# A third PSUM bank, taken from the projections' pair, for the chunked scan of a two-layer hybrid decoder

## The chip, the core and the metric

One core of one Trainium2 chip runs the whole program. The metric is device time in microseconds (us) of one execution. Engines are called PE (TensorE; PEld is its weight load), DVE (VectorE), ACT (ScalarE), POOL (GpSimd) and SP (SyncE, which issues the DMAs). Matmul results go into eight PSUM banks of 128 x 512 float32, named `B[0]` to `B[7]` in the kernel.

## The reference

Two layers over 512 tokens of width 1024. Each layer is

```
h   = rms_norm(x);  z, xbc, dt, sb_qkv, moba_qkv = split(h @ w_in)
xbc = silu(causal_conv(xbc));  dt = softplus(dt + bias);  xs, B, C = split(xbc)
per chunk c of 128 tokens, per head:
    y_diag  = ((C_c B_c^T) * L_c) (xs_c * dt_c)          # L_c: masked decays
    y_off   = (C_c state) * exp(acum_c)
    state   = state * chunk_decay_c + B_c^T (decay_to_end_c * dt_c * xs_c)
y_ssd = rms((y_diag + y_off + d_skip * xs) * silu(z)) * gain   # two groups
x  = x + rms_norm(concat(y_ssd, y_stickbreak, y_moba) @ w_out)
x  = x + rms_norm((silu(h2 @ w_gate) * (h2 @ w_up)) @ w_down), h2 = rms_norm(x)
```

The chunked scan (the Mamba-2 part, 8 heads of 64, two groups, state 128) runs over four chunks; the state is carried from chunk to chunk.

## The kernel before, in words

Every float32 projection is done as three matmul passes over a high and a low part of each operand; `split` makes these parts with one copy on ACT (L116) and one subtraction on DVE (L117). The weights come in 512 KB chunks through three raw buffers (DMA L131) and rings of four high and four low buffers (`wh`, `wl`).

All tiles are persistent; the eight banks are handed out by hand. A framework puts the instructions of each engine into an order at compile time, from priorities (program order, raised by `high_priority(offset=...)`) and simulated times. After that the order of an engine's queue is fixed; semaphores make an instruction wait for the data it reads, and for the earlier users of the bank or buffer it writes. So an instruction at the head of a queue that waits for a bank holds everything behind it on its engine.

The order of the work around the change, once in each layer:

- The MoBA attention (L431 to L464) writes logits into `B[3]`, their transposes into `B[4]` and its result into `B[2]`; L459 reads that out.
- The xBC projection (L475 to L482) and the Z projection (L483, matmuls at L212, silu on ACT at L156) take `B[0]` and `B[1]` in turn from the ring `acc`. Counting the takes of a layer (8 by the query-key pairs, 1 by dt, 8 by xBC), Z's token blocks 0 to 3 get `B[1]`, `B[0]`, `B[1]`, `B[0]`.
- The scan (L486 to L554), for each chunk c, takes banks from the ring `mx`: px (transposes of x, L501, read on DVE by L505, L506 and, but for the last chunk, L508), pb (transposes of B, L511, read by ACT L512; not in the last chunk), pc (C B^T, L515, read by L517), po (L531, read by L533; not in chunk 0) and pst (the state, L538, read by L541 or L544; not in the last chunk). That is 4, 5, 5 and 3 takes, 17 in all. The diagonal part (L525) always goes to `py = B[2]`, read by L527. L522 multiplies the decays by C B^T on DVE, L534 adds the two parts, L545 multiplies by silu(z), L549 squares on ACT, L164 takes a power on POOL, and L553 writes the chunk's result `MIX[c]`.
- The output projection (L559 to L591) works on token pairs with the banks `OB = (B[5:7], [B[7], B[0]], B[1:3], B[3:5])`. For token block j, `OB[j][0]` first holds the transposes of `MIX[j]`, `OB[j][1]` those of the attention results `MIXA[j]` (L577), which `split` moves to `RR`; then the matmuls of L565 accumulate in the two banks. So half of the matmuls of block j must wait until `MIX[j]` is done and its transposes have been read out. Pair 0 takes the weight chunks 4 to 7 first, then 0 to 3.
- Then comes the feed-forward part (L599 on): seven-product matmuls at L624, and the down projection at L691.

The scan has a priority offset of 100 instructions, the weight splits one of 800, the transposes for the output projection one of 4000.

Of the kernel before, what the change touches and what calls it, by code (L numbers as in the profile page):

```python
# [58 lines left out]
def trunk(ctx, tc, x, wch, wdt, gains, mixgain, conv, small, ident_d, consts_d, stack_d, out):  # L59
# [18 lines left out]
    B = [ps.tile([P, 512], F32, name=f"B{i}") for i in range(8)]  # L78
# [14 lines left out]
    def ring(items):  # L93
        n = [0]

        def take():
            n[0] += 1
            return items[(n[0] - 1) % len(items)]
        return take
# [171 lines left out]
    for l in range(DEPTH):  # L271
# [159 lines left out]
        mx = ring([B[3], B[4]])  # L431
# [51 lines left out]
        tok_proj(l, C_Z, acc, lambda t, p: silu(ZS[t], p))  # L483


        mx = ring(B[3:5])  # L486
        py = B[2]
        state = F[38]
        for c in range(NT):
# [281 lines left out]
```

## Time and profile before

| | |
|---|---|
| times of 3 runs | 1236.29, 1240.74 and 1318.46 us, median 1240.74 |
| profiled execution | 1236.18 us, its span 1234.4 us |
| mean granted clock of PE | 0.998 |
| busy in the span | PE 98%, PEld 88%, DVE 71%, ACT 49%, POOL 4% |

The profile is of one execution. Its span runs from the first to the last instruction; 1.8 us of its time lie outside. The third run, 1318.46 us, stands apart from the two others. Layer 0's scan lies at 186 to 236 us of the span, layer 1's at 794 to 844 us, with the same order of instructions.

### The profile page before, as it was taken

How to read it: one execution, taken by the hardware profiler on the slowest of the kernel's cores; microseconds unless marked ns; L12 is line 12 of the kernel's file. 1: busy time of each engine (PE TensorE's matmuls, PEld its weight loads, DVE VectorE, ACT ScalarE, POOL GpSimd, SP SyncE). 2: the span in 40 equal slices, each digit the busy share in tenths (PEclk: the TensorE clock that was granted, in tenths of full speed). 3: DMA queues.
4: the chain of work that ended last, by engine and by line, in shares of the span. 5: the costliest groups of instructions: out<-in, count | busy, mean ns of one | idle time of the engine just before them, and what ended most of it. 6: DMA issues, size and time to landing. Idle time of an engine off the chain costs nothing.

```text
span 1234.4 us, 19083 instructions
## 1 busy us (share of the span) xinstructions
PE 1206.0 (98%) x7558; PEld 1081.0 (88%) x7558; DVE 872.0 (71%) x1523; ACT 600.4 (49%) x1124; POOL 53.3 (4%) x88
## 2 busy tenths in 40 slices
PE   6999999999999999999999999999999999999997
PEld 5877888889999999888887888888899999998886
DVE  5456865879899998534555577478898899883343
ACT  5556664466444444433445666535654444453231
POOL 1010000010000000000110100001100000000000
PEclk9999999999999999999999999999999999999999
DMA  7322233242333333333323322132523333333321
GB/s 246 119 74 98 87 103 103 70 144 81 101 105 104 113 108 104 122 100 119 130 86 110 125 80 77 70 95 70 170 71 103 107 112 106 103 108 115 101 70 69
DMA packets 40778, 128.94 MB, mean 104 GB/s; under 512 B 5456, under 2 KB 5744, under 8 KB 40688
## 3 DMA queue, kind: packets, MB, share of 16 engines
q1 hardware_dynamic: 39344, 123.49, 30.6%
q0 software_dynamic: 1344, 4.23, 1.0%
q8 instruction: 59, 0.97, 0.3%
q14 instruction: 31, 0.25, 0.1%
HBM read 123.47 MB, written 4.23 MB: 103 GB/s over the span
## 4 chain that ended last, share of the span: by engine, by line
PE 81%; DVE 8%; DMA 5%; ACT 3%; issue 2%; POOL 0%; SPq 0%; DVEq 0%; POOLq 0%; ACTq 0%
PE B L624 22%; PE B L691 19%; PE B L221 15%; PE B L212 7%; PE B L565 6%; DMA wr<-in_wch_dram 4%; DVE wl L117 3%; ACT wh L116 2%; PE B L340 2%; DVE RR L650 1%; PE B L347 1%; PE B L453 1%; PE B L318 1%; PE B L525 1%; PE B L319 1%
## 5 line engine op out<-in xcount | busy, mean ns | idle before, releaser
L117 DVE TENSOR_TENSOR wl<-wr,wh 128x1024 fp32r<-128x1024 f32 (+1 forms) x198 | 220.0, 1114 | 85.8 <-ACT wh L116 84.4
L116 ACT ACTIVATE wh<-wr 128x1024 fp32r<-128x1024 f32 (+1 forms) x198 | 190.9, 966 | 151.3 <-PE B L624 88.0
L221 PE MATMUL B<-hT,wh 128*128 128x512 f32 (+1 forms) x768 | 215.7, 362 | 3.5 <-ACT F L307 2.2
L624 PE MATMUL B<-hT,wh 128*128 128x256 f32 x960 | 192.5, 283 | 0.6 <-ACT F L662 0.6
L624 PE MATMUL B<-D,wh 128*128 128x256 f32 x960 | 182.7, 283 | 0.6 <-DVE F L676 0.3
L691 PE MATMUL B<-wh,RR 128*128 128x512 f32 x608 | 164.8, 389 | 0.0
L624 PEld LDWEIGHTS B<-hT,wh 128*128 128x128 f32 x960 | 158.2, 192 | 1.0 <-ACT F L662 1.0
L221 PEld LDWEIGHTS B<-hT,wh 128*128 128x128 f32 x768 | 136.4, 191 | 23.6 <-ACT F L307 3.3
L624 PEld LDWEIGHTS B<-D,wh 128*128 128x128 f32 x960 | 153.2, 192 | 1.2 <-DVE F L676 0.7
L221 PE MATMUL B<-hT,wl 128*128 128x512 f32 (+1 forms) x384 | 137.7, 360 | 0.0
L624 PE MATMUL B<-hT,wl 128*128 128x256 f32 x480 | 136.2, 284 | 0.5 <-DVE wl L117 0.5
L624 PE MATMUL B<-D,wl 128*128 128x256 f32 x480 | 135.5, 283 | 0.0
L691 PEld LDWEIGHTS B<-wh,RR 128*128 128x128 f32 x608 | 114.0, 188 | 23.5
L116 ACT ACTIVATE wh<-RR 128x512 fp32r<-128x512 f32 (+1 forms) x120 | 85.8, 766 | 100.2 <-DVE RR L650 70.3
L117 DVE TENSOR_TENSOR RR<-F,RR 128x512 fp32r<-128x512 f32 x48 | 33.1, 691 | 103.7 <-ACT RR L116 103.7
L117 DVE TENSOR_TENSOR wl<-RR,wh 128x512 fp32r<-128x512 f32 (+1 forms) x120 | 101.1, 865 | 6.3 <-ACT wh L116 2.7
L691 PE MATMUL B<-wl,RR 128*128 128x512 f32 x304 | 95.4, 389 | 0.0
L624 PEld LDWEIGHTS B<-hT,wl 128*128 128x128 f32 x480 | 92.1, 192 | 1.0 <-DVE wl L117 1.0
L624 PEld LDWEIGHTS B<-D,wl 128*128 128x128 f32 x480 | 92.1, 192 | 0.0
L116 ACT ACTIVATE RR<-F 128x512 fp32r<-128x512 f32 x48 | 30.0, 629 | 125.9 <-PE B L691 124.7
L212 PE MATMUL B<-wh,hT 128*128 128x512 f32 x256 | 82.8, 399 | 0.9 <-DVE hT L117 0.9
L221 PEld LDWEIGHTS B<-hT,wl 128*128 128x128 f32 x384 | 73.0, 190 | 8.8
(206 smaller groups left out, 2004.3 us busy)
## 6 DMA issues: line engine op xcount, KB each, us to landing
wr<-in_wch_dram SPq DMA_DIRECT2D x204, 512.0 KB, 3.5
x<-in_x_dram SPq DMA_DIRECT2D x16, 256.0 KB, 3.2
F<-in_gains_dram SPq DMA_DIRECT2D x16, 256.0 KB, 4.4
F<-acd POOLq DMA_DIRECT2D x16, 256.0 KB, 6.3
xsave<-x SPq DMA_DIRECT2D x8, 256.0 KB, 2.0
x<-xsave SPq DMA_DIRECT2D x8, 256.0 KB, 3.3
out_dram<-x SPq DMA_DIRECT2D x8, 256.0 KB, 2.0
D<-in_mixgain_dram SPq DMA_DIRECT2D x4, 256.0 KB, 4.4
```

What stands on the lines that cost most here:

```text
L116: A.activation(hi, src, AF.Copy)
L117: return eng.tensor_tensor(lo, src, hi.bitcast(F32), op=OP.subtract)
L212: T.matmul(p, hT[a][:, k, t * P:(t + 1) * P], w[k // 2][b][:, (k % 2) * 512:(k % 2 + 1) * 512], start=n == 0, stop=n == 3 * KT - 1)
L221: T.matmul(p[:, t0 * P:t1 * P], w[b][:, k * P:(k + 1) * P], hT[a][:, k, t0 * P:t1 * P], start=first and n == 0, stop=n == 3 * KT - 1, skip ...
L318: T.matmul(p, tiles[2 + h][:, cs], tiles[h][:, cd], start=True, stop=False, skip_group_check=True)
L319: T.matmul(p, tiles[2 + h][:, cs], tiles[4 + h][:, cd], start=False, stop=stop, skip_group_check=True)
L340: T.matmul(pz[:, o:w], ntri if i2 == i else nones, s2, start=False, stop=i2 == NT - 1 and n == 1, skip_group_check=True)
L347: T.matmul(pv[:, j * 64:(j + 1) * 64], e[:, (j - i) * P:(j - i + 1) * P], VT[i][:, h * 64:(h + 1) * 64], start=i == NT - 1, stop=i == 0 an ...
L453: T.matmul(pv[:, h * 64:(h + 1) * 64], pTs[:, i * P:(i + 1) * P], VT[i][:, 256 + h * 64:256 + (h + 1) * 64], start=h == 0 and i == 0, stop ...
L565: T.matmul(OB[j][hf], lt, w[b][:, hf * 512:(hf + 1) * 512], start=k == ks[0] and a == 0 and b == 0, stop=k == ks[-1] and a == 1)
L624: T.matmul(p, w[b][:, half * 512 + k * P:half * 512 + (k + 1) * P], left(j, a, k), start=first and k == 0 and n == 0, stop=k == 3 and n == ...
L691: T.matmul(B[2 * t + hf], gs[a][:, t * P:(t + 1) * P], w[b][:, hf * 512:(hf + 1) * 512], start=i == 0 and a == 0 and b == 0, stop=i == HT ...
```

## The change

The ring that hands out banks to px, pb, pc, po and pst gets three banks instead of two:

```
-        mx = ring(B[3:5])
+        mx = ring([B[3], B[4], B[1]])
         py = B[2]
```

`B[1]` is one of the two banks of the ring `acc`, which the Z projection uses just before, and it is `OB[2][0]`, which takes the transposes of `MIX[2]` afterwards. No instruction is added or removed. What each take gets, in the order of the program:

```
chunk 0        px pb pc pst       before  3 4 3 4      after  3 4 1 3
chunk 1        px pb pc po pst    before  3 4 3 4 3    after  4 1 3 4 1
chunk 2        px pb pc po pst    before  4 3 4 3 4    after  3 4 1 3 4
chunk 3        px pc po           before  3 4 3        after  1 3 4
```

## Rows read from the trace of the kernel before

**Rows 1.** The page: span, busy times, and PE in 40 slices.

```profile
span 1234.4 us, 19083 instructions
...
PE 1206.0 (98%) x7558; PEld 1081.0 (88%) x7558; DVE 872.0 (71%) x1523; ACT 600.4 (49%) x1124; POOL 53.3 (4%) x88
...
PE   6999999999999999999999999999999999999997
```

**Rows 2.** Windows: stretch, length, busy us of PE PEld DVE ACT POOL, clock, DMA.

```profile
184.00:204.00 20.00, 20.00 (x116) 17.17 (x115) 8.24 (x13) 11.82 (x21) 0.17 (x1) 1.00 0.14 42
204.00:214.00 10.00, 10.00 (x59) 8.80 (x58) 8.57 (x14) 3.44 (x8) 1.52 (x2) 1.00 0.76 234
214.00:222.00 8.00, 8.00 (x51) 7.00 (x50) 6.67 (x11) 1.48 (x5) 0.00 (x0) 1.00 0.01 2
222.00:229.00 7.00, 6.10 (x42) 5.19 (x42) 7.00 (x15) 1.01 (x4) 1.07 (x1) 1.00 0.01 1
229.00:246.00 17.00, 17.00 (x90) 14.28 (x90) 13.93 (x23) 8.98 (x21) 1.40 (x2) 1.00 0.38 125
...
830.00:837.00 7.00, 6.14 (x42) 5.27 (x43) 7.00 (x15) 0.90 (x3) 1.07 (x1) 1.00 0.00 0
```

**Rows 3.** Waits of PE's weight loads, 184 to 246 us: us in total, times, longest.

```profile
PEld B L538 <- DVE F L517: 0.9, 1, 0.9
PEld B L531 <- DVE F L506: 0.5, 1, 0.5
PEld B L565 <- DVE RR L117: 0.3, 2, 0.2
PEld B L577 <- DVE F L517: 0.2, 1, 0.2
```

**Rows 4.** Timeline of PE, 222 to 229 us: start, us; idle before in brackets.

```profile
222.76 1.13 PE L538 MATMUL B<-D,D 128*128 128x256 f32 x4 [0.68 <-DVE F L517]
...
227.22 1.13 PE L531 MATMUL B<-D,F 128*128 128x256 f32 x4 [0.22 <-DVE F L506]
...
228.75 0.50 PE L565 MATMUL B<-wh,RR 128*128 128x512 f32 x1
```

**Rows 5.** Timeline of DVE and PE, 234 to 246 us: the last chunk and the last transposes.

```profile
235.03 0.68 DVE L533 TENSOR_TENSOR D<-B,SM 128x512 f32<-128x512 f32 x1
...
245.32 0.60 PE L577 MATMUL B<-ident,F 128*128 128x128 f32 x4
```

**Rows 6.** Timeline of DVE, 195 to 226 us.

```profile
195.75 0.42 DVE L517 TENSOR_TENSOR F<-B,cst 128x256 f32<-128x256 f32 x1 [3.54 <-PE B L515]
196.21 1.29 DVE L522 TENSOR_TENSOR F<-F,F 128x512 f32<-128x512 f32 x2
199.58 2.58 DVE L117 TENSOR_TENSOR wl<-wr,wh 128x1024 fp32r<-128x1024 f32 x2 [2.08 <-ACT wh L116]
...
214.23 0.69 DVE L533 TENSOR_TENSOR D<-B,SM 128x512 f32<-128x512 f32 x1 [1.19 <-PE B L531]
...
217.00 0.69 DVE L117 TENSOR_TENSOR RR<-B,RR 128x512 fp32r<-128x512 f32 x1 [0.69 <-ACT RR L116]
...
225.10 0.87 DVE L553 SCALAR_TENSOR_TENSOR F<-F,SM,D 128x256 f32<-128x256 f32 x2
```

**Rows 7.** Timeline, 195 to 207 us: bank users of chunks 0 and 1.

```profile
195.10 0.61 PE L515 MATMUL B<-F,F 128*128 128x128 f32 x4
...
197.12 0.60 ACT L156 ACTIVATE F<-B 128x512 f32<-128x512 f32 x1 [1.23 <-PE B L212]
...
200.94 0.61 PE L501 MATMUL B<-ident,F 128*128 128x128 f32 x4
...
201.80 0.39 ACT L512 ACTIVATE D<-B 128x256 f32<-128x256 f32 x1 [0.89 <-PE B L511]
...
202.41 0.68 DVE L505 TENSOR_TENSOR D<-B,SM 128x512 f32<-128x512 f32 x1
...
206.15 1.89 PE L525 MATMUL B<-D,F 128*128 128x64 f32 x16
```

**Rows 8.** Windows, columns as in rows 2, at a drop of the clock.

```profile
707.00:709.50 2.50, 1.30 (x6) 1.02 (x7) 1.83 (x2) 2.45 (x8) 0.00 (x0) 1.00 0.22 33
709.50:713.50 4.00, 4.00 (x12) 3.17 (x11) 2.14 (x3) 1.81 (x3) 0.00 (x0) 0.57 0.28 111
```

## Prediction

> **What bounds the kernel now.** I read first the page [rows 1]: PE is busy in 98% of the span, 1206.0 of 1234.4 us, and only its first and last slices fall below 9 tenths. The change neither adds nor removes an instruction, so PE's work stays; all that a bank can give back is time in which PE stands idle for want of one. Over the whole span PE is idle for 1234.4 - 1206.0 = 28.4 us, and most of that cannot belong to the scan, since the first and the last slice, of 30.9 us each, alone lack some 4 and 3 tenths, together about 20 us.
>
> The second view is busy time by stretch over the scan and the output projection of layer 0 [rows 2]. The reader should see that PE is full from 184 to 222 us and from 229 to 246 us, and that it lacks time only from 222 to 229 us: 6.10 of 7.00 us, while DVE is busy for all of the 7.00 us. Layer 1 shows the same at 830 to 837 us, 6.14 of 7.00 us. So the loss that the scan makes visible is 0.90 us in layer 0 and 0.86 us in layer 1, 1.8 us of the kernel.
>
> The third view is the waits of PE's weight loads in this stage [rows 3], which begin earlier than the matmuls and so count more: 0.9 + 0.5 + 0.3 + 0.2 = 1.9 us a layer. The timeline [rows 4] shows what the two largest are. L538 of chunk 2 (the state, bank 4) waits for L517 to read C B^T out of the same bank. L531 of chunk 3 (bank 3) waits for L506 to read px out of the same bank. Neither reads what L517 or L506 writes: these are waits for a bank and not for data. L577 (0.2 us) waits for bank 4 in the same way. The 0.3 us of L565 are waits for data, the split of the transposes.
>
> **The change part by part.**
>
> *The three bank waits go.* After the change, pst of chunk 2 goes to bank 4, whose user before is pb of the same chunk, and pc goes to bank 1; L538 reads what L512 makes out of pb anyhow, so its bank costs it nothing more. po of chunk 3 goes to bank 4 after L544 of chunk 2, whose result it needs anyhow. L577 for `MIXA[3]` must then wait for L533 of chunk 3 to free bank 4. That is at 235.03 + 0.68 = 235.7 us [rows 5], where it was ready at 228. Its result is wanted by pair 1, whose last transposes stand at 245.32 us [rows 5]; some 9 us of pair 0's matmuls hide the move, and if they did not, one split (0.69 us, the RR split in [rows 6]) would be bare. Removed are 0.9 + 0.5 + 0.2 = 1.6 us of weight-load waits a layer; by the matmuls' own rows it is 0.68 + 0.22 = 0.9 us [rows 4].
>
> *What is late next.* DVE. In 222 to 229 us it has no free moment [rows 2], and half of the matmuls of block 1 wait for `MIX[1]`, which L553 finishes at 225.10 + 0.87 = 226.0 us; its transposes and their split then start the matmuls at 228.75 us [rows 4, 6]. With the bank waits gone but `MIX[1]` no earlier, PE would reach that point sooner and wait there. So the gain is real only as far as DVE is moved forward, and DVE can move only into its own idle time before: 1.19 us ahead of L533, where it waits for L531 of chunk 1 [rows 6]. That L531 had bank 4 only after L512 had read pb; after the change, bank 4 is free for it when L508 has read px of chunk 1, and pb goes to bank 1. So this idle time is open to the change. The 0.69 us ahead of L117 [rows 6] waits for ACT and a transpose; it is not a wait for a bank and stays. Bounds of this part: at least 0 (everything is waited for at `MIX[1]`), at most 1.6 us a layer (all three bank waits). I take 1.2 us, the 1.19 us by which DVE can come forward, which lies between the matmuls' 0.9 and the weight loads' 1.6. Twice 1.2 is 2.4 us.
>
> *What the change delays.* pc of chunk 0 moves to bank 1, which Z's third block holds until its silu ends at 197.12 + 0.60 = 197.7 us [rows 7]; before, L515 ran at 195.10 us. It gets at least 2.6 us later. Queued behind it on DVE are L517 and the two L522 of chunk 0, 0.42 + 1.29 = 1.71 us [rows 6], whose result L525 reads at 206.15 us: 206.15 - 197.5 leaves over 8 us, and 6 us after the delay. Chunk 0's diagonal part has its cover. On PE nothing waits: Z's fourth block is there to be run, and bank 1 cannot be asked for before Z's third block has left PE. The cost falls on DVE: these 1.71 us leave a stretch in which it sits idle (3.54 us before, 2.08 us behind) and may land among the weight splits from 199.58 us on. From 197.7 us plus L515's own 0.61 us to 199.58 us there are still 1.3 us free. What does not fit is 1.71 - 1.3 = 0.4 us. I take nothing for it, because DVE's 1.19 us idle at 213 to 214 us comes behind it; the upper bound is the whole 1.71 us a layer.
>
> px of chunk 1 moves from bank 3 to bank 4, which is free only when L512 of chunk 0 has run, at 201.80 + 0.39 = 202.2 us, where L501 ran at 200.94 us [rows 7]. 1.3 us later; L505 behind it, 202.41 us, slips by about 1 us. What it makes is read by chunk 1's L525, behind 214 us. It costs nothing while DVE has a weight split to do in the meantime, and is inside the 1.71 us bound otherwise.
>
> The Trainium skill, on the page Perfetto Trace Analysis, section Optimizing Tensor Performance, says that independent matmul groups should rotate through different banks, so that reading one out overlaps the next group. By that rule alone every bank wait would turn into matmul time, and the sum would be 2 x 1.6 = 3.2 us; the row that has DVE at 7.00 of 7.00 us [rows 2] is what speaks against the whole of it here.
>
> *The sum.* 1236.18 us (the profiled execution: span 1234.4 and 1.8 around it) less 2.4 is 1233.8 us. The profiled execution lies under the middle of the two runs that agree, (1236.29 + 1240.74) / 2 = 1238.5, by 2.3 us; the shown median, 1240.74, is the upper one of these only because of 1318.46. On the footing of such runs: 1233.8 + 2.3 = 1236.1, say 1236 us.
>
> **The rivals.**
>
> *Another wait takes the place.* `MIX[1]` comes no earlier, and PE waits at its split for what it saved before. For: DVE at 7.00 of 7.00 us, and the chain through L527, L545, L549, POOL and L553 has no bank of the ring in it. Against: the 1.19 us of DVE idle time that is a bank's doing. Gain 0: 1238.5 us.
>
> *The bank is there in name only.* Of 17 takes six fall on bank 1 and the first must wait for Z; if the compile-time order stays as it is otherwise, what goes is the wait of L538 alone, 0.68 us a layer on PE [rows 4]. 1238.5 - 1.4 = 1237 us. It lies beside the forecast and is counted with the previous one.
>
> *Slower: the late pc pushes DVE's work into the full stretch.* Place: 197.7 to 214 us on DVE. Price: 1.71 us a layer, 3.4 us of the kernel, 1238.5 + 3.4 = 1242 us. It decides if the displaced L517 and L522 are put behind the weight splits and DVE's idle 1.19 us is used up by other work. Then `MIX[0]` and `MIX[1]` both come late, and the 0.9 us of PE's idle time in 222 to 229 us grows by as much. For: DVE has 8.57 of 10.00 us in 204 to 214 us [rows 2]. Against: 6 us of cover on PE.
>
> *The clock falls.* In layer 1 PE was busy for 1.30 of 2.50 us, and in the next 4 us the granted clock was 0.57 on average, a mix of full speed (2.4 GHz) and half (1.2 GHz) [rows 8]. In 222 to 229 us PE was busy for 6.10 of 7.00 us and the clock stayed 1.00 [rows 2]. If the new order put more idle time into one place, one such drop costs about 0.43 x 4 = 1.7 us; in each layer and beside the previous rival that is 1242 + 3.4 = 1245 us. The Trainium skill names such a thing, on the page TensorE: Matmul & The Clock Gate, section A second HAM failure mode: psum-queue depth-cycling: small idle times of PE between groups that cycle through banks make the clock swing. No row of the scan shows it.
>
> **How the numbers follow.** Forecast, a gain of 1 to 4 us: 0.50. Another wait, or a bank in name only, 1237 to 1239 us: 0.28. Slower by the late pc: 0.14. Clock: 0.03. The rest, 0.05, is that the compile-time order is made anew and something moves far from the scan, for which no row gives a price.
> The range takes in the largest gain, 1236.18 - 3.2 = 1233 us on the profile's footing, and the clock case, 1245 us; the two agreeing runs lie 2.2 us to either side of their middle, which I add at both ends: 1231 to 1247 us. A measurement of this kernel tells about 2% from no change, 25 us; none of the cases reaches that. I leave 0.02 for faster and 0.04 for slower, out of the last 0.05 and the spread that one run of 1318.46 us shows.
>
> **What would show each step.** Right: in the stage from 204 to 246 us no wait of L538 for L517 or of L531 for L506; L533 of chunk 1 without its 1.19 us of idle time before it; the matmuls behind the split of `MIX[1]` start at about 227.5 instead of 228.75 us; PE over 6.1 of 7 us in that stretch. The delay right: L515 of chunk 0 behind 197.7 us, L501 of chunk 1 behind 202.2 us, L525 of chunk 0 still near 206. The slower rival: L517 and L522 of chunk 0 behind the weight splits, and PE waiting for RR longer than 0.3 us. The prediction is wrong if the order of the queues differs in the feed-forward part, if the clock drops inside the scan, or if PE waits for bank 1 at the Z projection.

## The result, and the profile after

1245.43 us, the median of six runs (1243.32 to 1247.09), against 1237.12 us for the kernel before on the same chip: a ratio of 1.0066, 95% interval 1.0054 to 1.0079, in which the one run of 1318.46 us is left out as slow. The change costs some 8 us; I had forecast a gain of 1 to 4 us. The profiled execution took 1246.64 us, 10.5 us more than that of before. On the page, which answers to [rows 1], PE's busy time grew by 6.7 us with the same 7558 matmuls, so part of the loss is matmuls that ran slower and part is idle time.

```profile
span 1244.9 us, 19092 instructions
...
PE 1212.7 (97%) x7558; PEld 1086.6 (87%) x7558; DVE 871.3 (70%) x1523; ACT 600.2 (48%) x1124; POOL 54.4 (4%) x88
...
PEclk9999999999999999999999999998999999999999
```

I laid the two traces side by side by the starts of the same instructions. Layer 0 is 2.2 us late when Z begins (177.0 against 174.8 us). Some 1.7 us of that is a drop of the clock that before had at 709.7 us, in layer 1 [rows 8], and that fell at the same point of layer 0 here, at 103.2 us. The two drops about cancel over the whole kernel, and 2.2 us, called the shift below, is to be taken off when layer 0's scan is compared. What is left is in three places:

- From Z's start to the end of the output projection layer 0 takes 96.6 us instead of 94.7: +1.9 us.
- From layer 1's first convolution (718.6 before, 720.7 us after) to the end of its Z projection (812.0, 818.7): +4.6 us.
- From there to the end of layer 1's output projection (877.4, 888.1): +4.0 us.

**The scan of layer 0.** The windows of after that answer to [rows 2], in the same columns, cut finer behind 229 us.

```profile
204.00:214.00 10.00, 10.00 (x62) 8.78 (x61) 9.29 (x16) 4.50 (x11) 1.46 (x1) 1.00 0.83 267
...
222.00:229.00 7.00, 6.52 (x42) 5.65 (x39) 6.80 (x14) 0.91 (x4) 0.70 (x1) 1.00 0.01 2
229.00:233.00 4.00, 2.84 (x21) 2.41 (x22) 3.82 (x9) 1.41 (x5) 0.10 (x1) 0.99 0.00 0
233.00:236.40 3.40, 3.40 (x9) 2.66 (x9) 2.70 (x5) 1.84 (x2) 0.59 (x1) 0.51 0.00 0
```

DVE is still full; PE now lacks 1.16 of 4.00 us at 229 to 233 us, and for the 3.4 us behind that its clock is at half (0.51 of 2.4 GHz). The waits of PE, 184 to 246 us, answer to [rows 3] (us in total, times, longest):

```profile
PE B L525 <- DVE F L522: 1.1, 1, 1.1
PE B L577 <- DVE F L553: 0.5, 1, 0.5
```

The waits for banks (L538 for L517, L531 for L506) are gone, as forecast. Two waits for data stand in their place: the transposes of `MIX[1]` wait for L553, and chunk 3's L525 waits for its decays. Their place in PE's timeline (start, us; idle before in brackets):

```profile
229.06 0.83 PE L577 MATMUL B<-ident,F 128*128 128x128 f32 x4 [0.54 <-DVE F L553]
...
231.00 2.00 PE L525 MATMUL B<-D,F 128*128 128x64 f32 x16 [1.10 <-DVE F L522]
```

DVE's timeline over the same stretch answers to [rows 6]:

```profile
215.44 0.68 DVE L533 TENSOR_TENSOR D<-B,SM 128x512 f32<-128x512 f32 x1
...
218.03 0.68 DVE L505 TENSOR_TENSOR D<-B,SM 128x512 f32<-128x512 f32 x1
218.63 0.68 DVE L506 TENSOR_TENSOR F<-B,smal 128x512 f32<-128x512 f32 x1
219.22 0.68 DVE L508 TENSOR_TENSOR D<-B,SM 128x512 f32<-128x512 f32 x1
219.82 0.68 DVE L527 TENSOR_TENSOR F<-B,F 128x512 f32<-128x512 f32 x1
...
222.07 1.29 DVE L522 TENSOR_TENSOR F<-F,F 128x512 f32<-128x512 f32 x2
223.27 0.68 DVE L543 TENSOR_TENSOR D<-D,SM 128x512 f32<-128x512 f32 x1
223.87 0.69 DVE L545 TENSOR_TENSOR F<-F,F 128x512 f32<-128x512 f32 x1
...
228.53 0.87 DVE L553 SCALAR_TENSOR_TENSOR F<-F,SM,D 128x256 f32<-128x256 f32 x2
```

The same steps of DVE in the kernel before:

```profile
217.61 0.68 DVE L527 TENSOR_TENSOR F<-B,F 128x512 f32<-128x512 f32 x1
218.21 0.68 DVE L505 TENSOR_TENSOR D<-B,SM 128x512 f32<-128x512 f32 x1
...
220.72 0.69 DVE L545 TENSOR_TENSOR F<-F,F 128x512 f32<-128x512 f32 x1
...
223.29 1.29 DVE L522 TENSOR_TENSOR F<-F,F 128x512 f32<-128x512 f32 x2
```

L533 of chunk 1 has lost the 1.19 us of idle time ahead of it, as forecast, and starts at 215.44 - 2.2 = 213.2 instead of 214.23 us. But with a third bank chunk 2's px and pc are there earlier, and DVE's compiled order now takes up chunk 2 ahead of the last steps of chunk 1. The three reads of px (L505, L506, L508) stand ahead of chunk 1's L527, where before had L527 first; L527 itself is not late for that (219.82 - 2.2 = 217.6 us, as before). The two L522 and the L543 of chunk 2 stand ahead of chunk 1's L545, where before had them behind it: L545 starts at 223.87 - 2.2 = 221.7 instead of 220.72 us. `MIX[1]` is done at 228.53 + 0.87 = 229.4, or 227.2 us without the shift of 2.2: 1.2 us later than before (226.0), not 1.2 earlier; and `MIX[0]` is done at 217.5, or 215.3 us without the shift, 2.3 us later than before (213.0).

**The Z projection of layer 1**, far from anything that the change touches: windows, and PE's row.

```profile
800.70:803.00 2.30, 0.24 (x1) 0.05 (x1) 1.89 (x3) 2.30 (x5) 0.00 (x0) 0.99 0.19 51
803.00:806.40 3.40, 3.23 (x8) 2.58 (x9) 0.00 (x0) 1.09 (x3) 0.00 (x0) 0.50 0.00 0
```

```profile
803.17 0.80 PE L212 MATMUL B<-wh,hT 128*128 128x512 f32 x1 [2.23 <-ACT F L156]
```

Z's third block waits 2.23 us for `B[1]`, which the first block's silu has not read. ACT is late with it, since its table load for silu came late. ACT's view of L156 gives that load (last line; the second time is layer 1's), first before, then after:

```profile
L156 ACT ACT_TABLE_LOAD  x2: 1283/1283/1283, 183.2 to 791.0; - x2
```

```profile
L156 ACT ACT_TABLE_LOAD  x2: 1283/1283/1283, 185.4 to 797.1; - x2
```

It is 6.1 us later, with Z's start unmoved. Ahead of it stand the last exponentials of the MoBA attention, and the kernel itself ties the two: `silu` is issued `with after(order["exp"].values())` (L155), behind the last exponential of every group. PE's compiled queue differs from that of before around layer 0's scan, as it must, and then again in layer 1 from the attention on: at the first difference stick-breaking matmuls (L340) were put ahead of others (L318, L319) and of MoBA's L449. No bank of the ring is in that.

### The profile page after: what moved, and what is told of

The parts are those of the page before. It is cut to its first block, busy times and chain, and to the rows that moved or that the text cites. A ratio compares the mean times of both kernels' runs of the same rounds, so it can differ in the third digit from the quotient of the medians.

```text
span 1244.9 us, 19092 instructions
## 1 busy us (share of the span) xinstructions
PE 1212.7 (97%) x7558; PEld 1086.6 (87%) x7558; DVE 871.3 (70%) x1523; ACT 600.2 (48%) x1124; POOL 54.4 (4%) x88
## 4 chain that ended last, share of the span: by engine, by line
PE 88%; DVE 5%; ACT 3%; DMA 2%; issue 1%; POOL 0%; SPq 0%; DVEq 0%; POOLq 0%; ACTq 0%
PE B L624 29%; PE B L691 19%; PE B L221 15%; PE B L212 7%; PE B L565 7%; PE B L340 2%; PE B L347 1%; DVE wl L117 1%; PE B L525 1%; PE B L453 1%; DMA wr<-in_wch_dram 1%; ACT wh L116 1%; PE B L318 1%; PE B L319 1%; PE B L173 1%
## 5 line engine op out<-in xcount | busy, mean ns | idle before, releaser
L624 PE MATMUL B<-hT,wh 128*128 128x256 f32 x960 | 192.5, 283 | 0.6 <-ACT F L662 0.6
L624 PE MATMUL B<-D,wh 128*128 128x256 f32 x960 | 182.9, 283 | 0.1
L624 PEld LDWEIGHTS B<-hT,wh 128*128 128x128 f32 x960 | 158.1, 192 | 1.0 <-ACT F L662 1.0
L624 PEld LDWEIGHTS B<-D,wh 128*128 128x128 f32 x960 | 153.4, 192 | 0.7 <-DVE F L676 0.5
L624 PE MATMUL B<-hT,wl 128*128 128x256 f32 x480 | 136.2, 284 | 0.5 <-DVE wl L117 0.5
L624 PE MATMUL B<-D,wl 128*128 128x256 f32 x480 | 135.5, 283 | 0.0
L624 PEld LDWEIGHTS B<-hT,wl 128*128 128x128 f32 x480 | 92.0, 192 | 1.0 <-DVE wl L117 0.9
L624 PEld LDWEIGHTS B<-D,wl 128*128 128x128 f32 x480 | 92.1, 192 | 0.0
```

What stands on the lines that cost most here:

```text
L624: T.matmul(p, w[b][:, half * 512 + k * P:half * 512 + (k + 1) * P], left(j, a, k), start=first and k == 0 and n == 0, stop=k == 3 and n == ...
```

## The experiments

Theory A: the scan itself, through DVE's order and the clock that falls behind PE's new waits. Theory B: a new compile-time order in layer 1, passed on from layer 0's changed simulated times. Theory C, my slower rival: the late pc. D, E, G and I are named in the expectations as they come. Later H and J: whether it is DVE's load, or the banks, that takes the gain away.

**One layer at a time.**

```
-        mx = ring(B[3:5])
+        mx = ring([B[3], B[4], B[1]] if l == 0 else B[3:5])     # l0only
+        mx = ring([B[3], B[4], B[1]] if l == 1 else B[3:5])     # l1only
```

> Three banks in layer 0 alone; layer 1 has the two banks of before. In the profile of the changed kernel, layer 0's scan and output projection cost 1.9 us more than before, layer 1's Z projection 4.6 us and layer 1's scan and output projection 4.0 us. Theory A (the banks cost where they are used): about 1237 + 2 = 1239 us, layer 1 as before. Theory B (the new compile-time order of layer 0 moves the order of layer 1 too, and the loss at layer 1's Z projection comes from that, not from a bank): 1237 + 1.9 + 4.6 = 1243 to 1244 us, with a wait of some 2 us of L212 for ACT's L156 in layer 1 although no bank is changed there.

> Three banks in layer 1 alone. Theory A (the banks cost where they are used): 1237 + 4.6 + 4.0 = 1245 to 1246 us, with the wait of L212 for L156 in layer 1. Theory B (that wait comes from the order that layer 0 passes on): no such wait, and only the loss in the scan and output projection of layer 1 itself, 1.9 to 4.0 us: 1239 to 1241 us.

With layer 0 alone: 1243.8 against 1236.07 us, ratio 1.0072 [1.005, 1.0095], all of the loss. Layer 1, with two banks, has the late table load (795.7 us) and idles 2.64 us in Z. Up to there its PE queue has the order of after. The waiting line is another than I had expected: chunk 0's pc (L515) waits until px has been read out of the same bank (L508).

```profile
801.64 0.99 PE L515 MATMUL B<-F,F 128*128 128x128 f32 x4 [2.07 <-DVE D L508]
```

With layer 1 alone: 1237.4 us, 1.0016 [1.0002, 1.0029], under the 1239 to 1241 us that B had for it; no wait in Z, and a scan like that of layer 0 after the change: 1.64 us idle, then a drop, 96.7 us from Z to the output projection's end.

```profile
834.00:837.60 3.60, 2.13 (x16) 1.71 (x16) 3.60 (x8) 1.40 (x5) 0.00 (x0) 1.00 0.02 5
837.60:841.00 3.40, 3.40 (x13) 2.92 (x13) 2.56 (x6) 0.79 (x1) 0.69 (x1) 0.50 0.00 0
```

So a third bank in layer 0 alone disturbs layer 1 (B), and a scan with it takes about 2 us longer wherever it is (A).

**Where in the ring the third bank comes in.**

```
+        mx = ring([B[i] for i in (3, 4, 1, 4, 3, 4, 3, 4, 3, 4, 3, 4, 3, 4, 3, 4, 3)])   # pc0only
+        mx = ring([B[i] for i in (3, 4, 3, 4) + (3, 1, 4) * 5])                          # from_c1
```

> The banks of before for every take but one: pc of chunk 0 alone goes to bank 1, which Z's third block holds. Theory C (the late pc pushes L517 and the two L522 of chunk 0 into DVE's full stretch): L517 of chunk 0 after the weight splits, MIX[0] and MIX[1] later by 1 to 2 us, PE's idle time from Z's end to the end of the output projection 1.6 instead of 0.9 us a layer, and 1239 to 1242 us. Theory D (the loss is in the other moved takes, px of chunk 1 behind pb of chunk 0 on one bank above all): as before, 1237 us within 1 us, though pc is late.

> Chunk 0 has the banks of before (3 4 3 4), the third bank comes in from chunk 1 on. Theory C (the late pc of chunk 0 is the loss): the loss is gone, and what the third bank gives is left, 1234 to 1237 us. Theory D (the other takes): a loss of 2 us or more stays, 1239 us or above.

pc0only: 1235.46 against 1236.07 us, ratio 1.0005 [0.999, 1.002], no difference that the interval tells. pc is late as I had predicted (L515 at 202.9 instead of 195.1 us, of which 1.7 us are an earlier drop of the clock), `MIX[0]` comes 0.2 us later, and PE's idle time, 0.95 us a layer, is about that of before (0.90). The late pc by itself costs nothing that these runs can tell, and C falls. from_c1: 1237.61 us, 1.0013 [1.0, 1.0027]. Chunk 0 is as before; `MIX[1]` is some 1.4 us later, `MIX[2]` 6.5 us earlier, and PE waits in the two places of after, for less:

```profile
226.06 0.83 PE L577 MATMUL B<-ident,F 128*128 128x128 f32 x4 [0.67 <-DVE F L553]
...
227.99 2.00 PE L525 MATMUL B<-D,F 128*128 128x64 f32 x16 [0.54 <-DVE F L522]
```

Behind these the clock did not fall, and Z to the end of the output projection took 95.2 and 94.8 us. The time lies between what C (1234 to 1237 us) and D (1239 us or above) had for it. No gain here either.

**The order of layer 1, without touching a bank.** Transposes whose result nobody reads, behind layer 0's scan, move the simulated times. Each is some 0.11 us of PE; two_pad16 shows what they cost by themselves.

```
+        for _ in range(12 if l == 0 else 0):       # two_pad12; 16: two_pad16
+            T.transpose(B[1][:, 0:P], ident, ident)   # three_pad8: 8, with the change
```

> The two banks of before in both layers; twelve transposes of the identity into bank 1, which nobody reads, are added to layer 0 behind the scan. They take 12 x 0.11 = 1.3 us of PE and shift the compile-time order of layer 1 to the one of the changed kernel (a scan order as before, but the last softmax of MoBA behind Z's second block). Theory B (the order of layer 1 is the loss, and any small shift in layer 0 can bring it): 1236.5 + up to 1.3 + 4 to 6 = 1241 to 1244 us, with the wait of L212 for L156 of over 2 us in layer 1, though no bank is changed. Rival (the loss needs the third bank): 1236 to 1238 us.

> The same with sixteen transposes, 1.8 us of PE; here the compile-time order of layer 1 stays that of before. Both theories: 1236 to 1238.5 us, so that it shows what the added transposes cost by themselves.

> The whole change, three banks in both layers, with eight added transposes (0.9 us of PE) in layer 0; with them layer 1 gets the order of before ahead of the scan. Theory B: the wait of L212 for L156 is gone, only the two scans' losses are left, 2 us a layer: 1239 to 1242 us. Rival (the change costs 8 us by the banks): 1245 to 1247 us.

two_pad12: 1244.38 against 1237.99 us, 1.0053 [1.0035, 1.007], of which the transposes themselves are 1.3 us. Layer 1 has the other order, waits in Z as l0only did, and the clock falls behind it:

```profile
798.00:801.70 3.70, 1.44 (x8) 1.04 (x9) 1.95 (x4) 3.70 (x8) 0.00 (x0) 1.00 0.19 63
801.70:805.10 3.40, 3.40 (x10) 2.62 (x9) 1.66 (x3) 0.29 (x1) 0.00 (x0) 0.50 0.00 0
```

two_pad16, with more of them, keeps the order of before in layer 1: 1236.61 us, 0.9991 [0.9978, 1.0004]. three_pad8, the change with the order of before in layer 1, has no wait in Z: 1243.23 us, 1.0034 [1.0016, 1.0053], over the 1239 to 1242 us of theory B. Z to the end of the output projection takes 96.8 and 96.7 us, each with its drop of the clock; in layer 0 the transposes' 0.9 us are in it. The rest of its loss is partly its own: from layer 0's output projection to the first L624 it takes 29.9 us instead of 26.8, with 3.1 us of idle time instead of 1.6 and a drop at 289.5 us, and its order changed there too.

The start of layer 1's table load tells the two orders apart. It comes 14.8 us behind Z's start in after, l0only and two_pad12, and 8.3 or 8.4 us behind it in before, l1only, three_pad8 and three_hold.

**DVE's order in the scan.** three_hold is the change with the px reads of chunks 2 and 3 held until the chunk before has been through L545:

```
+                with after([done] if c > 1 else []):
                     V.tensor_tensor(r8(xdt), ...)    # L505, L506, L508
...
+                done = V.tensor_tensor(xd, xd, ZS[c], op=OP.mult)   # L545
```

> The whole change, with one more rule of order on DVE: the three reads of px of chunks 2 and 3 are queued behind the multiplication by silu(z) of the chunk before. Layer 1 keeps the order of before ahead of the scan. Theory E (the third bank lets chunks 2 and 3 in early, and full DVE does their reads ahead of the finish of chunk 1; MIX[1] late, PE idle twice in a row, clock down): MIX[1] 1 us or more earlier than in the changed kernel, PE's idle time at or under 0.9 us a layer, no drop of the clock in the scan, 1235 to 1237 us. Rival G (the loss is in chunk 0 and 1: px of chunk 1 behind pb on bank 4 makes MIX[0] 2 us late): MIX[0] still 2 us late, 2 us a layer stay, 1239 to 1241 us.

1239.89 against 1237.99 us, 1.0016 [1.0005, 1.0028]. `MIX[1]` came 1.4 us earlier than after the change, no drop in the scans, no wait in Z: so far theory E. But its time, 1235 to 1237 us, and its idle time, 0.9 us or less, did not come. The wait moved again, and PE's idle time in the stage rose to 2.67 us a layer (L568 is L565 and L520 is L517, three lines lower in this kernel; L502 is L501):

```profile
PE B L568 <- DVE RR L117: 1.7, 1, 1.7
...
PE B L502 <- DVE F L520: 1.0, 1, 1.0
```

The first is a wait for data; the second is a wait for a bank, since chunk 3's px takes `B[1]`, out of which L517 has first to read pc of chunk 2. Z to the end of the output projection: 96.1 us, still 1.4 us over before. `MIX[0]` is still 2.2 us late and the time lies in the range of rival G, so this run does not rule G out. z7_three (below) speaks against it as the whole cause: there `MIX[0]` is 1.0 us late and the stage loses more.

**A bank that is really free, and less work on DVE.** z7_three is the change with Z on `ring([B[7], B[0]])`, so that `B[1]` is free from the scan's first take. The three others leave work out.

```
-                V.tensor_tensor(r8(xd), r8(px), smal[:, 16:24]..., op=OP.mult)   # L506
-                V.tensor_tensor(xd, py, xd, op=OP.add)                           # L527
+                V.tensor_copy(xd, py)
```

> The whole change, but the Z projection takes banks 7 and 0 instead of 1 and 0, so that bank 1 is free for the scan from its start; layer 1 keeps the order of before ahead of the scan. Theory H (DVE is full in the scan, so a free bank only changes what DVE does first): 1237 to 1240 us, PE's idle time in the scan 0.9 us a layer or more. Rival I (a third bank pays as soon as it is free): PE's idle time under 0.9 us a layer and 1233 to 1236 us.

> The two banks of before, with less work for DVE: L506 (the skip term, four times 0.6 us a layer) is left out, and L527 copies instead of adding. The output lacks the skip term. MIX[1] earlier by 1 to 3 us, PE's idle time of 0.9 us a layer goes to under 0.5: 1235 to 1236.5 us.

> The whole change with the same work left out. Layer 1 keeps the order of before ahead of the scan. Theory H (the loss of 2 us a layer in the scan is DVE's full stretch and the clock drop that follows from it): with DVE relieved no drop of the clock in the scan, PE's idle time under 0.9 us, and within 1 us of the two-bank kernel with the same work left out. Rival J (the banks themselves cost, by their waits): 2 us a layer above it, 1239 to 1241 us.

> Three banks, Z on banks 7 and 0, and the same work left out: the case in which the third bank has the best chance. Theory H: 1 to 2 us under the two-bank kernel with the same work left out at most, since PE has under 1 us a layer to get back; rival J: above it.

z7_three: 1238.95 against 1236.4 us, 1.0018 [1.0008, 1.0029]. pc of chunk 0 is early (188.3 us), and PE idles 2.88 us a layer, all of it waits for DVE, without a drop of the clock in the scan. Z to the end of the output projection takes 97.1 and 97.0 us, more than after the change. So a bank that is free from the start does not pay (rival I falls). The waits in layer 0:

```profile
PE B L538 <- DVE D L508: 1.2, 1, 1.2
PE B L565 <- DVE RR L117: 1.1, 1, 1.1
PE B L577 <- DVE F L553: 0.5, 1, 0.5
```

With one read of px less for each chunk, the runs do not tell any variant from before: two_less 1236.29 us, 0.9997 [0.9986, 1.0009]; three_less 1236.07 us, 1.0002 [0.9992, 1.0011]; z7_three_less 1237.2 us, 1.0009 [0.9999, 1.002]. In three_less PE waits once, for chunk 3's decays and not for `MIX` (L524 and L521 are L525 and L522), and the clock stays up:

```profile
PE B L524 <- DVE F L521: 1.7, 1, 1.7
```

Z to the end of the output projection takes 94.7 us in two_less, 94.9 in three_less and 95.7 in z7_three_less. So relieving DVE removes the stage's loss with the change as it is, which is what H had, and leaves 1.0 of 2.3 us of it in z7_three_less; it gives no gain, with two banks or with three. My other expectations here missed: in two_less `MIX[1]` came 0.3 us later instead of 1 to 3 us earlier and PE idled 1.1 us a layer instead of under 0.5; in three_less it idled 1.70 us instead of under 0.9; z7_three_less came out over two_less and not under it.

## Why the prediction was wrong

**The bank waits** (1.6 us a layer): right as far as they go. All three are gone, and L533's idle 1.19 us with them. One count beside it was off: five of the 17 takes fall on bank 1, not six; no number of the sum hangs on it.

**What is late next**: the step that failed. I let DVE "be moved forward" by 1.19 us and counted that as 1.2 us a layer for `MIX[1]`. I had read DVE as full at 222 to 229 us [rows 2] and treated its order as given. A bank that comes free earlier changes what is ready first: DVE did start 1.0 us earlier at L533, but then took up chunk 2 (its reads, L522, L543), for which nobody waits yet, ahead of chunk 1's L545. The term measured -1.2 us instead of +1.2 us at `MIX[1]`, the matmuls behind its split start at 232.80 - 2.2 = 230.6 us where I had forecast 227.5, and PE's idle time in scan and output projection 1.64 us a layer instead of 0.90. three_hold shows that it isn't this one order alone: with `MIX[1]` put first, PE waits 1.7 us for a split and 1.0 us for a bank that DVE has still to read.

The rule of the Trainium skill that I had weighed there (Perfetto Trace Analysis, Optimizing Tensor Performance: rotate independent groups through different banks) gave a larger gain than I forecast. With the bank free from the start z7_three measured +0.18%; here the measurement decides against the rule. That reading out is what is short here is what DVE's 6.80 of 7.00 us and three_less point to.

**The late pc**, slower rival at 0.14: its delay came, with L517 and L522 of chunk 0 behind two weight splits as I had named it, its price did not (pc0only). The 6 us of cover that I had named held: L525 of chunk 0 starts at 208.61 - 2.2 = 206.4 instead of 206.15 us.

**The clock**, rival at 0.03: it came about inside both scans, and the size was right, 3.4 us at half speed or about 1.7 us each (6.8 us in layer 1 of the profiled execution). With 0.74 us more idle time (1.64 - 0.90) that makes 2.4 us a layer by the rows of PE; the stage grew by 1.9 to 2.0 us. The chance was wrong: I took the 1.00 of the row of before as evidence, though the forecast itself moved the waits. three_hold and z7_three keep the clock up and still lose 0.16 and 0.18%, so the clock isn't the whole of what a scan loses.

**Far from the scan**, 0.05 with no price: the second step that failed, a term that the sum put at nothing, and the larger part of the loss. l0only and two_pad12 show it without a change of bank in layer 1; l1only, three_pad8 and three_hold lack it. Up to the end of Z it is 2.6 to 2.8 us of waiting and one drop of 3.4 us, 1.7 us: some 4.5 us. It does not end there. From layer 1's first convolution to the end of its output projection, before takes 158.8 us, l0only 165.2 and two_pad12 166.6, both with two banks in that layer; 1.4 and 2.8 us of what is added lie behind Z. By the medians it costs some 5 to 6 us: l0only 7.7 us less 2 for its own scan, two_pad12 6.4 us less 1.3 for its transposes. At least two of my three signs of being wrong came: the clock drops inside the scan, and PE waits for bank 1 at a Z projection.

**The sum.** Two scans at 2 us and the order of layer 1 at 4.5 us make 8.5 of the measured 8.3 us. That this fits so well is partly luck. The same terms give 6.5 us for l0only, which measured 7.7, and 2 us for l1only, which measured 1.3; so layer 1's new order seems to cost more than 4.5 us, and a third bank on top of it to add less than 2, though the intervals do not exclude the sum. The profiles say the same: from the first convolution to the end of the output projection layer 1 takes 167.4 us in after, 1.7 of them by its longer drop, against 165.2 in l0only. In the profiled execution layer 1 has a drop of 6.8 us instead of 3.4 in its scan, hence 10.5 us there.

What stays open: why the clock falls behind the wait for the decays there and not in three_less, which simulated time tips the order in layer 1, how layer 1's loss divides between its order and its banks, and what the late `MIX[0]` costs (rival G). That the late table load is what PE waits for in Z is read from the traces and was not tried by moving the load alone. No version beat the kernel before.

## What to carry to other kernels

In this kernel a wait for a bank was not worth removing, since the engine that empties the bank had no room: more banks let it do later chunks' work earlier, and the chunk that was wanted next came late. Ask elsewhere what that engine will do next. Where the order of queues is made at compile time from simulated times, an edit of a few us can remake the order of a later layer; price that before believing a gain of 0.2%, and look in the new trace for the first place where the queues differ. Apply an edit to one layer at a time to tell the two apart.

## What was not expected of the hardware

The clock fell in all six profiled scans with the order of after in the scan (after in both layers, layer 0 of l0only, layer 1 of l1only, three_pad8 in both layers), for 3.4 us in all but one, five times behind waits of some 0.5 and 1.1 us, 2 us apart. In layer 0 of three_pad8, where added transposes (L558) run among the first of them, it fell behind the wait for L522 alone:

```profile
229.94 2.27 PE L525 MATMUL B<-D,F 128*128 128x64 f32 x16 [1.23 <-DVE F L522]
```

It did not fall behind the longer wait for the same decays in three_less, 1.7 us, nor in the scans of three_hold and z7_three, where PE idled 2.67 and 2.88 us in all. In layer 1 of after the drop was twice as long (length 6.80 us, clock 0.50), with PE busy throughout:

```profile
838.00:844.00 6.00, 4.36 (x32) 3.60 (x30) 5.79 (x12) 1.62 (x7) 0.70 (x1) 0.99 0.00 0
844.00:850.80 6.80, 6.80 (x25) 6.03 (x25) 4.61 (x9) 1.93 (x4) 0.70 (x1) 0.50 0.01 2
```

So the length of a wait, or the idle time of a stage, does not tell whether the clock falls; what else does was not settled. The drop early in a layer (103.2 us after, 709.7 us before) goes with none of the changes: pc0only and two_less have it in both layers, z7_three in neither, and in layer 0 it lies ahead of everything that the change moves. It is taken here for a matter of the execution: some 1.7 us that a comparison of two single profiles must take out first.
